# One of four weight sums per FFN block pair: made by adding transfers instead of by VectorE

## Chip, cores and metric

The kernel runs on one core of a Trainium2 chip. The metric is device time in microseconds (us) of one execution, as the median of several runs. VectorE is DVE in the profile, ScalarE is ACT, GpSimd is POOL, SyncE is SP, TensorE is PE (its weight loads PEld).

## The reference

One layer of a streaming encoder on x (512 tokens x 1024 features), all in float32. First a mixing sub-layer with three attention branches, which the change does not touch. Then the feed-forward network (FFN):

```
h = rmsnorm(x, g_ffn_pre)
gu = h @ w_ffn_in                                  # 1024 x (2 * 2816)
f = (silu(gu[:, :2816]) * gu[:, 2816:]) @ w_ffn_out
x = x + rmsnorm(f, g_ffn_post)
```

## The kernel before, in words

**Precision.** Each float32 operand is split into a high part (rounded to fp32r) and a low part (the rest). `split` (L73 to L75) makes them: ACT casts the high part (L74), DVE subtracts it from the source (L75). `passes` (L81 to L87) makes each product in three matmuls: high x high (L85), high x low (L86), low x high (L87).

**FFN, first matmul.** The 2816 columns of each half of w_ffn_in are cut into 22 blocks of 128. Block j of the gate half (g) and block j of the other half (u) make a pair; one pair is one row block of f. Pairs 0 to 2 are computed directly (`ffn`, L932). For pairs 3 to 21, 19 in all, `blocks` (L919) and `seven` (L886) use seven products instead of eight for the 2 x 2 block product of (g, u's two halves of the contraction) with the two halves of the tokens. Each product has four contraction chunks of three matmuls, so 84 matmuls per pair, each with 256 moving columns.

**The left sides** of the seven products come from `left_sides(j)` (L851). It loads g (512 KB, tag `wraw`, three buffers) and u (512 KB, tag `lraw`, two buffers), each 128 partitions x (8 contraction chunks x 128 columns), by SP's DMA queue. h[0] and h[1] are the first and last 512 columns, that is chunks 0 to 3 and 4 to 7. DVE makes four sums of 128 x 512 (L871): s12[h0] = u[h0] + u[h1]; s12[h1] = s12[h0] - g[h0]; s34[h0] = g[h0] - u[h0]; s34[h1] = g[h1] - s12[h1]. s12 and s34 are tiles of the tag `wl`, which has two buffers. Then g, s12 and s34 are split as a whole (128 x 1024) into tiles of 2048 columns (tag `w2`, four buffers, `wide` at L109), and u[h1] into a tile of tag `wh`. Split g gives products 1 and 2, split s12 gives 5 and 6, split s34 gives 7 and 3, split u[h1] gives 4.

**Order of the products.** `blocks` interleaves two pairs. In the steady stretch PE runs, per period: products 1 and 5 of pair j, 7 of pair j-1, 2 and 6 of pair j, 4 of pair j-1, 3 of pair j. Products 1, 2 and 3 read h2 itself (names bank<-h,w in the trace), 5, 6 and 7 read sums of h2 (bank<-act,w), 4 reads the `wh` tile (bank<-act,wh). Between them ACT copies banks out (L893, L895, L900) and DVE adds them (L898, L903, L907), and multiplies (L908, L911). Products 7 and 4 share a bank: product 4 may start when L907 has read it.

**What sets the order.** PE's order is the program's, written out by hand. For the FFN the order of the other engines' instructions and of the DMAs on each queue is set by the build's scheduler, from the dependencies and from when it expects a buffer to be free; each engine and each queue then runs in that order. A tile's buffer is free for its next use when every reader of the tile is done: s12's when ACT's cast and DVE's subtraction of it have ended.

**Before the stage.** `mix_out` (L785) ends the mixing sub-layer: post-norm, then the rows are transposed and split into h2 (L79 is DVE's part of that split, L359 the transpose on PE). The last of these transposes run inside `ffn`, beside the products of pair 0. POOL then adds the parts of h2 (L839) for the right sides of products 4 to 7. POOL has no work in the steady stretch of the stage.

Of the kernel before, what the change touches and what calls it, by code (L numbers as in the profile page):

```python
# [14 lines left out]
OP = mybir.AluOpType  # L15
AX = mybir.AxisListType

P = 128
# [4 lines left out]
DFF = 2816  # L23
# [24 lines left out]
class Layer:  # L48
# [802 lines left out]
    def left_sides(self, j):  # L851

        nc = self.nc
        g = self.load(self.a["w_ffn_in"][:, j * P:j * P + P], NK, P, "wraw")[0]
        u = self.load(self.a["w_ffn_in"][:, DFF + j * P:DFF + j * P + P], NK, P, "lraw")[0]
        x, h = {}, (slice(0, 512), slice(512, 1024))

        def cut(t, n, ps):
            for i, p in enumerate(ps):
                x[p] = tuple(t[:, c:c + 512] for c in (512 * i, n + 512 * i))  # L860

        def both(src, *ps):
            t = self.wide()
            self.split(t[:, 0:1024], t[:, 1024:2048], src)
            cut(t, 1024, ps)

        both(g, 1, 2)
        s12, s34 = self.big("wl", F32), self.big("wl", F32)
        for t, c, a, b, op in ((s12, 0, u[:, h[0]], u[:, h[1]], OP.add), (s12, 1, s12[:, h[0]], g[:, h[0]], OP.subtract),
                               (s34, 0, g[:, h[0]], u[:, h[0]], OP.subtract), (s34, 1, g[:, h[1]], s12[:, h[1]], OP.subtract)):  # L870
            nc.vector.tensor_tensor(t[:, h[c]], a, b, op=op)  # L871
        both(s12, 5, 6)
        both(s34, 7, 3)
        t = self.big("wh")
        self.split(t[:, h[0]], t[:, h[1]], u[:, h[1]])
        cut(t, 512, (4,))
        return x
# [123 lines left out]
```

## Time and profile before

| | us |
|---|---|
| median of 3 runs (912.41 to 913.62) | 912.44 |
| the profiled execution | 910.88 |
| its span, first to last instruction | 909.1 |
| seven-product stage in the trace, about | 592 to 781 |
| second matmul of the FFN (w_ffn_out), about | 781 to 897 |

All durations below come from the profiled execution. Its span is shorter than its time by what lies around the first and last instruction. Times in the trace count from the start of the span. "Idle before" in brackets names what the engine was waiting for. A DMA row of SPq shows the time in which SP issued the transfer, not the transfer.

### The profile page before, as it was taken

How to read it: one execution, taken by the hardware profiler on the slowest of the kernel's cores; microseconds unless marked ns; L12 is line 12 of the kernel's file. 1: busy time of each engine (PE TensorE's matmuls, PEld its weight loads, DVE VectorE, ACT ScalarE, POOL GpSimd, SP SyncE). 2: the span in 40 equal slices, each digit the busy share in tenths (PEclk: the TensorE clock that was granted, in tenths of full speed). 3: DMA queues.
4: the chain of work that ended last, by engine and by line, in shares of the span. 5: the costliest groups of instructions: out<-in, count | busy, mean ns of one | idle time of the engine just before them, and what ended most of it. 6: DMA issues, size and time to landing. Idle time of an engine off the chain costs nothing.

```text
span 909.1 us, 13518 instructions
## 1 busy us (share of the span) xinstructions
PE 888.3 (98%) x5146; PEld 780.1 (86%) x5146; DVE 641.5 (71%) x1120; ACT 458.6 (50%) x808; POOL 117.1 (13%) x153
## 2 busy tenths in 40 slices
PE   8999999999999999999999999899999999999997
PEld 7888888888888888888788888899999999888885
DVE  6589999953688976787563478788888887932215
ACT  6465674332666665666353355455555555811111
POOL 2000000020132304433212123400000000000000
PEclk9999999999999999999999999999999999999999
DMA  6523543454354433222483624213333334533002
GB/s 203 173 83 117 168 111 93 127 128 116 104 156 112 128 82 92 70 59 58 140 252 107 185 83 127 71 47 95 115 109 102 114 97 139 164 97 106 29 1 92
DMA packets 129541, 101.17 MB, mean 111 GB/s; under 512 B 4652, under 2 KB 115292, under 8 KB 129476
## 3 DMA queue, kind: packets, MB, share of 16 engines
q1 hardware_dynamic: 128884, 99.26, 37.9%
q10 hardware_dynamic: 592, 1.05, 0.3%
q8 instruction: 40, 0.66, 0.3%
q14 instruction: 25, 0.20, 0.1%
HBM read 93.73 MB, written 2.12 MB: 105 GB/s over the span
## 4 chain that ended last, share of the span: by engine, by line
PE 82%; DVE 10%; issue 3%; ACT 2%; POOL 2%; DMA 1%; POOLq 0%; DVEq 0%; ACTq 0%
PE bank L85 19%; PE bank L86 19%; PE bank L87 19%; PE bank L745 15%; DVE wl L75 3%; PE bank L545 2%; PE bank L560 1%; PE bank L179 1%; PE bank L178 1%; PE bank L209 1%; PE bank L211 1%; PE bank L210 1%; DMA lraw<-in_w_ffn_in_dram 1%; DVE e L632 1%; POOL rs L241 1%
## 5 line engine op out<-in xcount | busy, mean ns | idle before, releaser
L75 DVE TENSOR_TENSOR wl<-wraw,wh 128x1024 fp32r<-128x1024 f32 (+1 forms) x112 | 128.5, 1149 | 101.3 <-ACT wh L74 101.0
L74 ACT CAST wh<-wraw 128x1024 fp32r<-128x1024 f32 (+1 forms) x112 | 107.2, 959 | 139.3 <-PE bank L86 74.7
L85 PE MATMUL bank<-h,wh 128*128 128x512 f32 (+1 forms) x376 | 149.0, 396 | 0.0
L87 PE MATMUL bank<-h,wl 128*128 128x512 f32 (+1 forms) x376 | 145.4, 387 | 1.0 <-DVE wl L75 0.9
L86 PE MATMUL bank<-h,wh 128*128 128x512 f32 (+1 forms) x376 | 145.1, 386 | 0.0
L745 PE MATMUL bank<-w,act 128*128 128x512 f32 x360 | 89.0, 394 | 0.0
L87 PEld LDWEIGHTS bank<-h,wl 128*128 128x128 f32 x376 | 70.6, 188 | 15.8 <-DVE wl L75 1.7
L85 PEld LDWEIGHTS bank<-h,wh 128*128 128x128 f32 x376 | 71.0, 189 | 11.6 <-issue 0.2
L86 PEld LDWEIGHTS bank<-h,wh 128*128 128x128 f32 x376 | 70.9, 188 | 11.5
L745 PEld LDWEIGHTS bank<-w,act 128*128 128x128 f32 x360 | 67.4, 188 | 14.9
L745 PE MATMUL bank<-wh,act 128*128 128x512 f32 x240 | 72.5, 393 | 0.0
L85 PE MATMUL bank<-act,wh 128*128 128x256 f32 (+1 forms) x204 | 69.3, 340 | 0.7 <-DVE s L907 0.7
L86 PE MATMUL bank<-act,wh 128*128 128x256 f32 (+1 forms) x204 | 68.0, 334 | 0.0
L87 PE MATMUL bank<-act,w 128*128 128x256 f32 x228 | 64.2, 282 | 0.0
L86 PE MATMUL bank<-act,w 128*128 128x256 f32 x228 | 64.2, 281 | 0.0
L87 PE MATMUL bank<-h,w 128*128 128x256 f32 x228 | 64.2, 281 | 0.0
L86 PE MATMUL bank<-h,w 128*128 128x256 f32 x228 | 64.2, 281 | 0.0
L85 PE MATMUL bank<-act,w 128*128 128x256 f32 x228 | 64.2, 281 | 0.0
L85 PE MATMUL bank<-h,w 128*128 128x256 f32 x228 | 64.2, 281 | 0.0
L241 POOL TENSOR_TENSOR rs<-ms,mhalf 128x1 f32<-128x1 f32 x18 | 11.6, 646 | 387.4 <-DVE ms L240 383.7
L609 POOL TENSOR_TENSOR p<-toep,score 128x128 f32<-128x128 f32 (+3 forms) x32 | 30.4, 963 | 200.2 <-DVE score L518 102.9
L745 PEld LDWEIGHTS bank<-wh,act 128*128 128x128 f32 x240 | 45.0, 188 | 9.8
(190 smaller groups left out, 2109.5 us busy)
## 6 DMA issues: line engine op xcount, KB each, us to landing
wraw<-in_w_in_dram SPq DMA_DIRECT2D x64, 512.0 KB, 3.7
lraw<-in_w_ffn_in_dram SPq DMA_DIRECT2D x22, 512.0 KB, 4.0
wraw<-in_w_ffn_in_dram SPq DMA_DIRECT2D x22, 512.0 KB, 3.7
wraw<-in_w_ffn_out_dram SPq DMA_DIRECT2D x11, 512.0 KB, 3.5
lraw<-in_w_ffn_out_dram SPq DMA_DIRECT2D x11, 512.0 KB, 3.5
wraw<-in_w_mem_kv_dram SPq DMA_DIRECT2D x8, 512.0 KB, 3.7
lraw<-in_w_out_dram SPq DMA_DIRECT2D x6, 512.0 KB, 5.5
wraw<-in_w_out_dram SPq DMA_DIRECT2D x6, 512.0 KB, 3.9
```

Source lines behind the costliest of these rows:

```text
L74: self.nc.scalar.copy(hi, src)
L75: (eng or self.nc.vector).tensor_tensor(lo, src, hi.bitcast(F32), op=OP.subtract)
L85: self.nc.tensor.matmul(out, lhsT=sh, rhs=mh, start=first and i == 0, stop=False, **kw)
L86: self.nc.tensor.matmul(out, lhsT=sh, rhs=ml, start=False, stop=False, **kw)
L87: self.nc.tensor.matmul(out, lhsT=sl, rhs=mh, start=False, stop=last and i == n - 1, **kw)
L178: self.nc.tensor.matmul(out, lhsT=x, rhs=y[:, 0:n], start=True, stop=False)
L179: self.nc.tensor.matmul(out, lhsT=x, rhs=y[:, T:T + n], start=False, stop=True)
L209: self.nc.tensor.matmul(ps, lhsT=ah[:, s], rhs=wh[:, k2], start=st, stop=False)
L241: self.nc.gpsimd.tensor_tensor(r, ms, self.mhalf, op=OP.pow)
L545: self.nc.tensor.transpose(ps[:, c:c + P], p[i][:, j * P:(j + 1) * P], self.ident)
L609: nc.gpsimd.tensor_tensor(s, toep[0][:, 0:n][:, ::-1], self.mask[i], op=OP.add)
L745: self.nc.tensor.matmul(ps[c], lhsT=st_[:, s], rhs=mv_[:, 0, c * 512:(c + 1) * 512], start=f and k == order[0], stop=l and k == order[-1])
```

## The change

The first of the four sums, s12[h0] = u[h0] + u[h1], is no longer made by DVE. Chunks 0 to 3 of u are read a second time from w_ffn_in, on SP's queue, straight into s12[h0] (256 KB). Two transfers on POOL's queue then read chunks 4 and 5, and 6 and 7, of u from w_ffn_in (128 KB each), and add them into the two halves of s12[h0] in the on-chip buffer. u is still loaded whole as before, since s34[h0] and the split of u[h1] read it. The other three sums stay on DVE.

```diff
         s12, s34 = self.big("wl", F32), self.big("wl", F32)
-        for t, c, a, b, op in ((s12, 0, u[:, h[0]], u[:, h[1]], OP.add), (s12, 1, s12[:, h[0]], g[:, h[0]], OP.subtract),
+
+        for q, k, o, n, how in ((nc.sync, 0, 0, 4, {}), (nc.gpsimd, 4, 0, 2, {"accum_op": OP.add}),
+                                (nc.gpsimd, 6, 256, 2, {"accum_op": OP.add})):
+            q.dma_start(s12[:, o:o + n * P].rearrange("p (k c) -> p k c", c=P),
+                        self.a["w_ffn_in"][k * P:(k + n) * P, DFF + j * P:DFF + j * P + P]
+                        .rearrange("(k p) c -> p k c", p=P), **how)
+        for t, c, a, b, op in ((s12, 1, s12[:, h[0]], g[:, h[0]], OP.subtract),
                                (s34, 0, g[:, h[0]], u[:, h[0]], OP.subtract), (s34, 1, g[:, h[1]], s12[:, h[1]], OP.subtract)):
             nc.vector.tensor_tensor(t[:, h[c]], a, b, op=op)
```

## Rows read from the trace of the kernel before

**Rows 1.** The page, busy time of each engine.

```profile
PE 888.3 (98%) x5146; PEld 780.1 (86%) x5146; DVE 641.5 (71%) x1120; ACT 458.6 (50%) x808; POOL 117.1 (13%) x153
```

**Rows 2.** Windows: stretch; us, each engine's busy us (instructions), granted clock, DMA share, GB/s.

```profile
640.00:649.92 9.92, 9.92 (x86) 9.92 (x86) 8.44 (x14) 5.42 (x9) 0.00 (x0) 1.00 0.35 106
...
570.00:572.00 2.00, 0.00 (x0) 0.00 (x0) 2.00 (x4) 0.60 (x2) 0.00 (x0) 1.00 0.30 90
```

**Rows 3.** Waits of PE, 520 to 909 us: total us, times, longest.

```profile
PE bank L359 <- DVE h L79: 4.4, 2, 2.9
PE bank L85 <- DVE s L907: 0.7, 1, 0.7
```

**Rows 4.** Line 871, the removed sum, 540 to 600 us and 600 to 775 us.

```profile
L871 DVE TENSOR_TENSOR wl<-lraw x3: 689/692/694, 554.7 to 598.2; 128x512 f32<-128x512 f32 x3
...
L871 DVE TENSOR_TENSOR wl<-lraw x16: 691/693/695, 606.7 to 755.5; 128x512 f32<-128x512 f32 x16
```

**Rows 5.** Timeline of DVE, one period: start, duration, instruction, idle before.

```profile
645.16 1.22 DVE L75 TENSOR_TENSOR w<-wl,w 128x1024 fp32r<-128x1024 f32 x1
646.41 0.69 DVE L871 TENSOR_TENSOR wl<-lraw 128x512 f32<-128x512 f32 x1
...
649.42 0.69 DVE L871 TENSOR_TENSOR wl<-wl,wraw 128x512 f32<-128x512 f32 x1
...
652.52 0.43 DVE L907 TENSOR_TENSOR s<-bank,s 128x256 f32<-128x256 f32 x1 [1.21 <-PE bank L87]
...
654.88 0.42 DVE L898 TENSOR_TENSOR silu<-bank,s 128x256 f32<-128x256 f32 x1
655.21 1.22 DVE L75 TENSOR_TENSOR w<-wl,w 128x1024 fp32r<-128x1024 f32 x1
```

**Rows 6.** Timeline of ACT, the cast of the same s12.

```profile
644.06 1.05 ACT L74 CAST w<-wl 128x1024 fp32r<-128x1024 f32 x1 [0.41 <-PE bank L87]
```

**Rows 7.** Timeline of PE: first matmul of a product 5, and of a product 4.

```profile
649.49 0.28 PE L85 MATMUL bank<-act,w 128*128 128x256 f32 x1
...
655.15 0.28 PE L85 MATMUL bank<-act,wh 128*128 128x256 f32 x1
```

**Rows 8.** Timeline of SP's queue, the two issues of the same period.

```profile
644.93 0.37 SPq L95 DMA_DIRECT2D wraw<-in_w_ffn_in_dram  x1
649.53 0.37 SPq L95 DMA_DIRECT2D lraw<-in_w_ffn_in_dram  x1
```

**Rows 9.** DMA issues of the whole run: count, KB each, median us to landing.

```profile
wraw<-in_w_ffn_in_dram SPq DMA_DIRECT2D x22, 512.0 KB, 3.7
...
lraw<-in_w_out_dram SPq DMA_DIRECT2D x6, 512.0 KB, 5.5
...
wraw<-in_w_up_c_dram SPq DMA_DIRECT2D x8, 256.0 KB, 2.8
...
out_dram<-fin SPq DMA_DIRECT2D x4, 256.0 KB, 2.0
```

**Rows 10.** Timeline of POOL, 540 to 580 us: its longest and its shortest instruction there.

```profile
541.30 3.31 POOL L75 TENSOR_TENSOR act<-lraw,act 128x1024 fp32r<-128x1024 f32 x1 [2.48 <-ACT act L74]
...
551.76 0.55 POOL L241 TENSOR_TENSOR rs<-ms,mhalf 128x1 f32<-128x1 f32 x1
```

**Rows 11.** Timeline of DVE, subtractions of s12 of pair 4 and of pair 21.

```profile
596.93 1.23 DVE L75 TENSOR_TENSOR w<-wl,w 128x1024 fp32r<-128x1024 f32 x1 [0.58 <-ACT w L74]
...
764.20 1.22 DVE L75 TENSOR_TENSOR w<-wl,w 128x1024 fp32r<-128x1024 f32 x1
```

**Rows 12.** Timelines of DVE and of POOL where the FFN begins.

```profile
563.73 1.22 DVE L75 TENSOR_TENSOR w<-wl,w 128x1024 fp32r<-128x1024 f32 x1
...
569.25 0.69 DVE L871 TENSOR_TENSOR wl<-lraw 128x512 f32<-128x512 f32 x1
...
572.26 0.87 DVE L79 SCALAR_TENSOR_TENSOR h<-bank,cols,h 128x256 fp32r<-128x256 f32 x2
...
572.82 2.53 POOL L839 TENSOR_TENSOR act<-h 128x512 f32<-128x512 f32 x2 [6.21 <-DVE h L79]
```

## The prediction, made before the result was known

> **What bounds the kernel now.** I read the page's busy times first, then the waits of PE, then one block pair of the FFN stage engine by engine. On the page the reader is to see PE busy over 98% of the span [rows 1]; since the ends of matmuls are modelled, that alone says little, so the stage itself has to show whether PE ever waits. The window of one block pair in the steady stretch is 9.92 us long; PE is busy for all of it, DVE for 8.44, ACT for 5.42, POOL for nothing, the DMA engines for 0.35 [rows 2]. A block pair is 7 products of 4 x 3 matmuls, and 84 matmuls in 9.92 us are 0.118 us each, back to back. The list of PE's waits from the post-norm stage to the end confirms it: 0.7 us behind one VectorE addition (L907), and 4.4 us behind the splits of h (L79) where the FFN begins [rows 3]. So in the stage that the change edits, PE sets the time, and DVE work taken away there is worth nothing by itself. What can matter is whether the operands of the products still come in time.
>
> **What is removed.** The 128x512 addition u0+u1 (L871, output half 0 of s12) runs 3 times before 600 us and 16 times after, 19 in all [rows 4]. It costs 0.69 us each, 13 us of DVE. I cost this at nothing in the steady stretch: PE's 9.92 us per block pair hide it, and DVE had 1.48 us to spare per block pair already. If that cover went (if PE were faster), it would be worth at most 0.69 us per pair.
>
> **What is added, and where it queues.** Per block pair: a 256 KB read on SP's queue into half of the s12 buffer, then two accumulating transfers of 128 KB each on POOL's queue, which must wait for that read, and only then the second sum s12-g0, the cast and the subtraction that make the operands of product 5. The new thing is a loop through one buffer. The wl tag has two buffers, s12 and s34, so s12 of the next pair can be written only when the split of the present s12 has ended. Today that shows in the DVE timeline: the subtraction of s12 runs from 645.16 to 646.38, and the addition for the next pair starts at once, at 646.41 [rows 5]. Today the loop then has time: the second sum comes at 649.42, ACT's cast of an s12 at 644.06 [rows 6] and so of the next one 9.92 later, and the subtraction at 655.21 [rows 5]. PE first uses the result at 649.49 for the one that ended at 646.38 [rows 7]: 3.11 us of slack.
>
> How long may the loop be? The subtraction of s12 for the second seven-product pair starts at 596.93, that of the last at 764.20 [rows 11]; ends 598.16 and 765.42, 167.26 us for 17 loops. With the 3.11 us of slack, 170.4 us are free: 10.02 us per loop. Everything above it is paid 17 times.
>
> **The loop, term by term.** *Read.* A 256 KB weight load of just this form (four 512-byte rows per partition, w_up) lands 2.8 us after its issue, a 512 KB one 3.7 [rows 9], so 0.9 us belongs to 256 KB more. SP issues the load of a later g at 644.93 [rows 8], 1.45 us before the read can go; that load lands near 648.6, and the read's data comes behind it on the same queue: 648.6+0.9 = 649.5, which is 3.15 us after 646.38. Bounds 2.8 and 3.7; I take 3.15.
>
> *Accumulating transfers.* No transfer issued by POOL and none that adds is in this trace, so both parts are bounded. Issue: below, SP's 0.37 us [rows 8]; above, POOL's longest instruction, 3.31 us; I take its shortest, 0.55 us [rows 10], as an issue moves no data itself, and count it twice. Landing: below, 2.0 us as the shortest 256 KB row shows (a store); above, 5.5 us as the slowest weight load; I take 2.8 us, the 256 KB load, because an adding transfer of 128 KB reads 128 KB of weights and 128 KB of the buffer [rows 9]. SP issues a 512 KB load at 649.53 [rows 8], right beside them: I add 0.9 us, half of what such a load takes beyond the fixed part. Sum 2x0.55+2.8+0.9 = 4.8 us if the two overlap; bounds 2x0.37+2.0 = 2.7 and 2x3.31+5.5 = 12.1.
>
> The page "DMA: Bandwidth & Descriptors" of the Trainium skill (section "Anatomy of one DMA") fits a GpSimd-issued transfer as 2.0 us plus its bytes over 436 GB/s, so an estimate of 2.3 us for 128 KB; no run here shows it, and with it in place of 2.8+0.9 the loop would be 9.95 us and the sum of the change nothing.
>
> *Tail.* Second sum 0.69, then 1.10 from the start of the cast to the start of the subtraction (644.06 to 645.16), then 1.22: 3.0 us at least [rows 5, 6]. Above: if DVE keeps today's order, all that stands from the second sum at 649.42 to the end of the subtraction at 656.43, less the 1.21 us idle in it: 5.8 us [rows 5]. I take 3.4: the 0.42-us addition that stands right ahead of the subtraction today (654.88) stays there, the rest fits elsewhere.
>
> Loop: 3.15+4.8+3.4 = 11.35 us. 17 x 11.35 = 192.95, less 170.4: **22.6 us lost on PE**, as waits in front of product 5.
>
> **What waits behind the new waits.** On SP the read waits for DVE's subtraction; behind it stands the load issued now at 649.53, which comes later than the read anyway: nothing. On DVE the second sum waits for POOL's transfers; behind it stands L907 (652.52), whose end at 652.95 PE needs only at 655.15 [rows 5, 7]: 2.2 us of cover per pair, and once PE itself is late this cover grows: nothing more. On POOL nothing else runs in the stretch. The DMA engines' share of 0.35 for 1 MB per pair grows by at most 0.75 MB (with the buffer reads) to some 0.6: no bound. PE's clock: in a window where PE did nothing for 2 us the granted clock stays at 1.00, the 2.4 GHz level [rows 2]; I add nothing for stalls of 1 to 2 us.
>
> **Start of the stage.** The 4.4 us that PE waited for h L79 end behind five DVE instructions of the second pair (569.25 to 572.26), of which the removed addition is the first [rows 3, 12]: a gain of 0.6 us, and 1.8 if the two sums that need s12 fall behind L79 as well. Against this, s12's buffer there is free at 564.95 (563.73+1.22), the read lands at 568.1, the additions at 572.9; were the second sum still ordered ahead of L79, L79 would start 1.3 us later than now. POOL is idle for 6.21 us before its own additions at 572.82 [rows 12], so the two issues fit. I take zero, between -1.8 and +1.3.
>
> **The sum.** The profiled execution took 910.88 us (span 909.1 and 1.8 around it): 910.88+22.6 = 933.5. The median of the runs is 1.56 higher, 912.44, so 935.0 us.
>
> **Rivals.** (1) *No loss, the other side.* If the two transfers land within 3.45 us of the read (10.02-3.15-3.4), the loop hides under PE, and nothing moves but the start of the stage: 912.4, between 910.6 and 913.7. For it: 2.7 us is the lower bound, and stores land in 2.0. Against: the additions are two, behind a read, beside a 512 KB load. The point that decides is 3.45 us. The estimate from the Trainium skill's page above leads here, too. (2) *Faster.* The same, and in the start of the stage DVE reaches L79 1.8 us earlier and the 0.7 us at L907 goes as well: 909.9. For it: PE's idle time there is real and DVE-bound. Against: it needs the scheduler to put three instructions behind L79. (3) *A longer loop.* DVE keeps today's order around the second sum (5.8 for 3.4): loop 13.75, 17x13.75-170.4 = 63, so 976. Or the second transfer starts only when the first has landed, 2x(0.55+2.8)+0.9 = 7.6 for 4.8: loop 14.15, 70 us, so 983. For it: both go to one queue and one tile. Against: they write different columns, and the instruction order is set anew at build, with the transfers in it. With the upper bound of 12.1 us it would be 1059; I give that next to nothing, as no load here is near it but one group.
>
> **How the numbers follow.** Forecast (a loop of 10.2 to 12.8 us, 915 to 960) 0.49; rival 3, 0.21; rival 1, 0.22; rival 2, 0.08. A difference under 0.2% (1.8 us) cannot be told from none in this kernel. So faster 0.08, same 0.22, slower 0.70. The range goes from 910.5, which holds rival 1, to 972, which leaves out rival 2 and over half of rival 3: two in ten.
>
> **What would show it.** Right: the subtractions of s12 (DVE, w from wl) stand some 11.4 us apart instead of 9.92; PE's waits show 17 of over a microsecond behind L75; DVE idles before the second sum, released by a transfer into wl; the read lands about 3.1 us after its issue, the adding ones within 4.8 of it. Wrong: PE has no wait in the stage (rival 1), or loops of over 13 us (rival 3), where the two landings one after the other or the DVE order tell which. A clock below 1.00 in the stretch would be a cost that I left out.

## The result, and the profile after

The changed kernel takes 1019.36 us (1018.25 to 1021.01), against 912.42 us before on the same chip: a ratio of 1.118 (95% interval 1.115 to 1.120), 106.9 us more. The forecast was slower, 935 us, in a range of 910.5 to 972; the loss is nearly five times the 22.6 us forecast.

The page of the changed kernel: busy times, the queue of POOL's transfers, and the new issues (KB each, median us from issue to landing).

```profile
PE 926.6 (91%) x5146; PEld 814.4 (80%) x5146; DVE 627.6 (62%) x1101; ACT 453.8 (45%) x808; POOL 160.9 (16%) x191
...
q0 software_dynamic: 10336, 4.98, 4.0%
...
wl<-in_w_ffn_in_dram SPq DMA_DIRECT2D x19, 256.0 KB, 3.7
wl<-in_w_ffn_in_dram POOLq DMA_DIRECT2D x38, 128.0 KB, 3.5
```

Against [rows 1] DVE has lost 14 us of work, as the edit says, and PE is busy for 38 us longer with the same 5146 matmuls. POOL's transfers are no load worth the name: 4.0% of the DMA engines' time. So the loss is waiting, and a slower PE. The waits of PE from 540 to 890 us (total, times, longest):

```profile
PE bank L87 <- DVE w L75: 65.8, 18, 5.1
PE bank L359 <- DVE h L79: 5.5, 1, 5.5
PE bank L86 <- DVE h L79: 2.7, 1, 2.7
```

Where [rows 3] had one wait of 0.7 us behind L907 and nothing else in the steady stretch, there is now one wait per pair behind L75. One loop of the s12 buffer, from the end of one subtraction to the end of the next, in the timelines of SP, POOL, DVE and ACT (new line numbers: L872 the transfers, L877 the sums, L913 and L914 what were L907 and L908):

```profile
683.71 1.22 DVE L75 TENSOR_TENSOR w<-wl,w 128x1024 fp32r<-128x1024 f32 x1
...
683.88 0.37 SPq L95 DMA_DIRECT2D wraw<-in_w_ffn_in_dram  x1
684.96 0.37 SPq L872 DMA_DIRECT2D wl<-in_w_ffn_in_dram  x1
...
690.08 1.21 POOL L872 DMA_DIRECT2D wl<-in_w_ffn_in_dram  x1 [11.40 <-DVE act L914]
693.87 1.22 POOL L872 DMA_DIRECT2D wl<-in_w_ffn_in_dram  x1 [2.58 <-issue]
...
697.60 0.69 DVE L877 TENSOR_TENSOR wl<-wl,wraw 128x512 f32<-128x512 f32 x1 [8.04 <-DMA wl<-in_w_ffn_in_dram]
698.21 1.22 DVE L75 TENSOR_TENSOR w<-wraw,w 128x1024 fp32r<-128x1024 f32 x1
...
698.45 1.04 ACT L74 CAST w<-wl 128x1024 fp32r<-128x1024 f32 x1 [8.80 <-DVE wl L877]
...
700.28 1.22 DVE L75 TENSOR_TENSOR w<-wl,w 128x1024 fp32r<-128x1024 f32 x1
```

The reader is to follow the links, each of which starts when the one before ends. The subtraction of s12 ends at 684.93, SP issues the read at 684.96; POOL issues the first adding transfer at 690.08, the second at 693.87; the second sum runs at 697.60; the next subtraction ends at 701.50. That is 16.57 us where [rows 5] has 10.05 us (646.38 to 656.43), and it is in three parts: 5.1 us until POOL's first issue, 7.5 us for the two additions, 3.9 us for the tail. On DVE the subtraction of g (698.21) stands behind the waiting second sum, and product 1 of the next pair waits for that: PE's wait names L75.

Two things in these rows mislead. POOL's first issue is put down to L914, since several semaphores are waited for and that one came last. In the loops where the trace gives the read's landing, 10 of 17, POOL starts 0.63 to 0.72 us after it (here landing 4.4 us after the issue, 689.36, and 0.72 us more), while L914 ends 0.4 us ahead of POOL's start in one loop, 15 us ahead in another, and in a third is still running: it is the read. And the 2.58 us ahead of the second issue end by nothing that the profile shows ("issue"); in the program that instruction has no wait at all, and DVE is idle from 689.55 to 697.60. The first transfer lands 3.5 us after its issue at 690.08, so at 693.6, and the second issue follows 0.3 us later; it does so in all 17 loops.

The second sums of the steady stretch, with the time of the first and the last of 17, give the mean period: (871.3-617.4)/16 = 15.87 us.

```profile
L877 DVE TENSOR_TENSOR wl<-wl,wraw x17: 691/693/693, 617.4 to 871.3; 128x512 f32<-128x512 f32 x17
```

By the prediction's own account 17 loops of 15.87 us less the 170.4 us that are free are 99.4 us. The rest, some 7 us, has to come from before the first loop. The two traces show both parts in one line each: PE's matmuls of L85 in products 1, 2 and 3, with the start of the first and of the last, before and after the change.

```profile
L85 PE MATMUL bank<-h,w x228: 280/281/282, 591.4 to 776.7; 128*128 128x256 f32 x114
...
L85 PE MATMUL bank<-h,w x228: 275/282/421, 599.7 to 884.1; 128*128 128x256 f32 x114
```

The stage starts 8.3 us late, and from there takes 284.4 us in place of 185.3: 99.1 us more.

### The profile page after: what moved, and what is told of

Its sections match the earlier page's. It is cut to its first block, busy times and chain, and to the rows that moved or that the text cites. A ratio compares the mean times of both kernels' runs of the same rounds, so it can differ in the third digit from the quotient of the medians.

```text
span 1016.7 us, 13672 instructions
## 1 busy us (share of the span) xinstructions
PE 926.6 (91%) x5146; PEld 814.4 (80%) x5146; DVE 627.6 (62%) x1101; ACT 453.8 (45%) x808; POOL 160.9 (16%) x191
## 3 DMA queue, kind: packets, MB, share of 16 engines
q0 software_dynamic: 10336, 4.98, 4.0%
## 4 chain that ended last, share of the span: by engine, by line
PE 61%; DVE 14%; DMA 11%; issue 8%; POOL 4%; ACT 2%; DVEq 0%; POOLq 0%; ACTq 0%
PE bank L745 14%; PE bank L87 13%; PE bank L85 13%; PE bank L86 12%; DMA wl<-in_w_ffn_in_dram 9%; DVE w L75 3%; DVE wl L75 3%; POOL wl L872 2%; DVE wl L877 2%; PE bank L545 2%; PE bank L560 1%; PE bank L179 1%; PE bank L178 1%; PE bank L209 1%; PE bank L211 1%
## 5 line engine op out<-in xcount | busy, mean ns | idle before, releaser
L75 DVE TENSOR_TENSOR wl<-wraw,wh 128x1024 fp32r<-128x1024 f32 (+1 forms) x112 | 128.6, 1149 | 101.5 <-ACT wh L74 101.1
L85 PE MATMUL bank<-h,wh 128*128 128x512 f32 (+1 forms) x376 | 149.0, 396 | 0.0
L87 PE MATMUL bank<-h,w 128*128 128x256 f32 x228 | 74.4, 326 | 65.4 <-DVE w L75 65.4
L87 PEld LDWEIGHTS bank<-h,w 128*128 128x128 f32 x228 | 50.6, 222 | 68.9 <-DVE w L75 68.9
L74 ACT CAST w<-wl 128x1024 fp32r<-128x1024 f32 x38 | 39.6, 1046 | 140.4 <-DVE wl L877 139.4
L877 DVE TENSOR_TENSOR wl<-wl,wraw 128x512 f32<-128x512 f32 x19 | 13.1, 692 | 120.1 <-DMA wl<-in_w_ffn_in_dram 115.8
L872 POOL DMA_DIRECT2D wl<-in_w_ffn_in_dram x38 | 46.4, 1222 | 252.2 <-DMA wl<-in_w_ffn_in_dram 108.6
L85 PEld LDWEIGHTS bank<-h,wh 128*128 128x128 f32 x376 | 71.0, 189 | 11.7 <-issue 0.2
L85 PE MATMUL bank<-act,w 128*128 128x256 f32 x228 | 71.6, 314 | 0.0
L86 PE MATMUL bank<-act,w 128*128 128x256 f32 x228 | 70.7, 310 | 0.0
L87 PE MATMUL bank<-act,w 128*128 128x256 f32 x228 | 70.0, 307 | 0.4 <-DVE w L75 0.4
L85 PE MATMUL bank<-act,wh 128*128 128x256 f32 (+1 forms) x204 | 69.2, 339 | 1.1 <-DVE s L913 1.1
L86 PE MATMUL bank<-h,w 128*128 128x256 f32 x228 | 70.1, 307 | 0.0
L85 PE MATMUL bank<-h,w 128*128 128x256 f32 x228 | 69.9, 306 | 0.0
```

The lines of the kernel that those rows point to most:

```text
L74: self.nc.scalar.copy(hi, src)
L75: (eng or self.nc.vector).tensor_tensor(lo, src, hi.bitcast(F32), op=OP.subtract)
L85: self.nc.tensor.matmul(out, lhsT=sh, rhs=mh, start=first and i == 0, stop=False, **kw)
L86: self.nc.tensor.matmul(out, lhsT=sh, rhs=ml, start=False, stop=False, **kw)
L87: self.nc.tensor.matmul(out, lhsT=sl, rhs=mh, start=False, stop=last and i == n - 1, **kw)
L872: q.dma_start(s12[:, o:o + n * P].rearrange("p (k c) -> p k c", c=P), self.a["w_ffn_in"][k * P:(k + n) * P, DFF + j * P:DFF + j * P + P] . ...
```

## The experiments

The theory after the result (A in the expectations): a loop through the s12 buffer, in which the second adding transfer is held back until the first has landed, plus some 8 us at the start of the stage. The rivals are given with each run. Runs that needed room on the chip moved four tiles of the attention stage (`score0` to `score3`, `diag`) to a pool that is closed before the FFN; the last experiment is the control for that.

**More room for the descriptors of POOL's transfers.**

```diff
-    nc = bacc.Bacc("TRN2", target_bir_lowering=False, num_devices=1, dynamic_dma_scratch_size=1024)
+    nc = bacc.Bacc("TRN2", target_bir_lowering=False, num_devices=1, dynamic_dma_scratch_size=4096)
```

> The changed kernel with four times the on-chip memory for the descriptors of POOL's transfers (4096 bytes per partition for 1024); the score and diag tiles move to the pool that is closed before the FFN, to make room. Theory A (the second adding transfer is held until the first has landed, for want of room for its descriptors): the 2.6 us between the end of the first issue and the start of the second fall to under 0.3 us, the loop of 16.6 us shortens to 14.0, and the time falls by 17 x 2.6 = 44 us to about 975 us. Rival B (POOL's transfers go one after the other whatever the room): the gap stays at 2.6 us and the time at 1019 us.

Measured: 970.44 us, ratio 1.065 (1.063 to 1.066). The timeline of POOL shows both issues as one piece of 2.44 us, without a gap; below it are the second sums of the stretch and the matmuls of L85.

```profile
699.06 2.44 POOL L872 DMA_DIRECT2D wl<-in_w_ffn_in_dram  x2 [11.40 <-DVE s L913]
...
L877 DVE TENSOR_TENSOR wl<-wl,wraw x17: 691/693/694, 609.4 to 825.0; 128x512 f32<-128x512 f32 x17
...
L85 PE MATMUL bank<-h,w x228: 276/281/420, 594.6 to 836.7; 128*128 128x256 f32 x114
```

The period is (825.0-609.4)/16 = 13.48 us, 2.4 us shorter, and the time is 48.9 us shorter. The gap was the room for descriptors. Of what is left, 58.3 us, the account puts 17 x 13.48 - 170.4 = 58.8 us into the loops. The trace has 56.8 us there (242.1 for 185.3) and 3.2 us ahead of the stage, together the 60.2 us between the two profiled executions (971.03 and 910.88). So 5.1 us of the gain come from the start of the stage.

**Plain transfers in place of adding ones.**

```diff
-        for q, k, o, n, how in ((nc.sync, 0, 0, 4, {}), (nc.gpsimd, 4, 0, 2, {"accum_op": OP.add}),
-                                (nc.gpsimd, 6, 256, 2, {"accum_op": OP.add})):
+        for q, k, o, n, how in ((nc.sync, 0, 0, 4, {}), (nc.gpsimd, 4, 0, 2, {}),
+                                (nc.gpsimd, 6, 256, 2, {})):
```

> The two transfers on POOL's queue overwrite instead of adding, so s12[h0] holds chunks 4 to 7 of u and not the sum. Theory A (room for descriptors: an adding transfer needs two reads for each write, a plain one one): the second issue follows the first within 0.3 us, the loop is 16.6 - 2.6 = 14.0 us or, if a plain transfer also lands sooner (2.8 for 3.6), 13.2, and the time 960 to 978 us. Rival B (any two transfers of POOL follow one another): gap 2.6 us, 1005 to 1020 us.

Measured: 945.75 us, ratio 1.038 (1.035 to 1.041), better than either theory said. Timeline of POOL, the sums, the issues with their landing, and the queue of POOL's transfers:

```profile
699.75 1.44 POOL L872 DMA_DIRECT2D wl<-in_w_ffn_in_dram  x2 [11.09 <-DMA wl<-in_w_ffn_in_dram]
...
L877 DVE TENSOR_TENSOR wl<-wl,wraw x17: 691/693/694, 606.6 to 796.8; 128x512 f32<-128x512 f32 x17
...
wl<-in_w_ffn_in_dram POOLq DMA_DIRECT2D x38, 128.0 KB, 2.7
...
q0 software_dynamic: 1824, 4.98, 1.8%
```

With the small room of the changed kernel there is no gap, as theory A has it, so it is the adding form that fills the room. The last line shows how the forms differ: the same bytes go in 1824 packets, 48 for each of the 38 transfers, where the adding ones took 10336, 272 each. Two costs of adding that I had not priced come on top: the issue takes 1.22 us for an adding transfer and 0.72 for a plain one, and the landing 4.0 us (overlapped, in the run before) for 2.7. The period is 11.89 us: 17 x 11.89 - 170.4 = 31.7 us, measured 33.6. In the trace the matmuls of L85 run from 592.8 to 808.8 us, so 30.7 us are lost in the stage and 1.4 ahead of it.

**A third buffer for s12 and s34.**

```diff
-    BUFS = dict(h=8, act=22, wraw=3, wh=2, wl=2, lraw=2, pt=3, fin=4)
+    BUFS = dict(h=8, act=22, wraw=3, wh=2, wl=3, lraw=2, pt=3, fin=4)
```

> The changed kernel with three wl buffers for two (the same tiles moved to make room, descriptor memory as in the changed kernel). Theory A (the loss is the loop through the one s12 buffer): a read can go some 7.7 us earlier, when the buffer of the s34 before is free, so 17.7 us are free for a loop of 16.6: no wait of PE behind L75 in the steady stretch, granted clock 1.00, and 912 to 922 us, the remainder being the start of the stage. Rival B (the transfers themselves, their load on the DMA engines or POOL's issue cost the time): PE goes on waiting, over 960 us.

Measured: 1000.26 us, ratio 1.097 (1.095 to 1.099): theory A's bounds missed by 78 us, and rival B's met. The chain of waits of this kernel, one loop in order of time (start, us, what; some short links are left out):

```profile
697.30 1.13 DVE w L75
...
698.46 2.93 DMA wl<-in_w_ffn_in_dram
...
702.07 5.16 DMA wl<-in_w_ffn_in_dram
707.23 3.83 issue
711.06 0.20 DVE wl L877
...
711.67 0.41 DVE act L917
712.09 1.14 DVE w L75
...
713.25 3.03 DMA wl<-in_w_ffn_in_dram
```

and the second adding transfer of that loop in the timeline of POOL, which the chain has inside the 3.83 us of "issue":

```profile
707.55 1.22 POOL L872 DMA_DIRECT2D wl<-in_w_ffn_in_dram  x1 [4.27 <-issue]
```

The chain has no PE in it: it is still a loop of buffer, read, additions and DVE, of 14.8 us. The read now goes into the buffer of the s34 before; but that s34's subtraction (712.09 in the next round) stands on DVE behind the second sum that waits for the transfers (711.06). The order of DVE's instructions closed the loop again, one tile further on. So a spare buffer is not yet a decoupling, and the run could not tell A from B. It does show two things by itself. The gap follows the landing: the first adding transfer takes 5.2 us to land here, at 707.23, and the second is issued 0.3 us after that, with a gap of 4.27 us for 2.58. And the read, here no longer right behind a load of 512 KB on SP's queue, lands after 2.9 us; in the changed kernel, 1.1 us behind such a load, its median is 3.7.

**A tile of its own for the transfers.** Three buffers of 128x512, filled by the read and the additions; s12 keeps its second half alone.

```diff
+        wa = self.late.tile([P, 512], F32, name="wa", tag="wa", bufs=3)
...
-            q.dma_start(s12[:, o:o + n * P].rearrange("p (k c) -> p k c", c=P),
+            q.dma_start(wa[:, o:o + n * P].rearrange("p (k c) -> p k c", c=P),
...
-        for t, c, a, b, op in ((s12, 1, s12[:, h[0]], g[:, h[0]], OP.subtract),
+        for t, c, a, b, op in ((s12, 1, wa, g[:, h[0]], OP.subtract),
...
-        both(s12, 5, 6)
+        t = self.wide()
+        self.split(t[:, 0:512], t[:, 1024:1536], wa)
+        self.split(t[:, 512:1024], t[:, 1536:2048], s12[:, h[1]])
+        cut(t, 1024, (5, 6))
```

> The changed kernel, but the read and the two adding transfers fill a tile of their own (128x512, three buffers) in place of the half of s12; s12 keeps only its second half, and its split is made in two halves. Same transfers, same room for descriptors. Theory A (the loss is a loop in which a buffer has to be given back before its next transfers start, and three buffers of their own put the transfers two pairs ahead): 29.8 us are free for read and additions of about 12 us, no wait of PE behind L75 in the steady stretch, sums 9.92 us apart, 908 to 925 us, where all above 912 comes from POOL's queue at the start of the stage. Rival B (two adding transfers per 9.92 us load POOL or the DMA engines too much): periods of over 11 us, over 930 us.

Measured: 939.28 us, ratio 1.030 (1.029 to 1.032). The number is rival B's, the trace is not. The waits of PE from 300 us on, the timeline of POOL around 490 us, far ahead of the FFN, and the matmuls of L85:

```profile
PE bank L85 <- ACT wh L74: 18.0, 1, 18.0
PE bank L359 <- DVE act L251: 6.9, 1, 6.9
...
486.42 1.21 POOL L873 DMA_DIRECT2D wa<-in_w_ffn_in_dram  x1 [2.69 <-issue]
490.23 1.22 POOL L873 DMA_DIRECT2D wa<-in_w_ffn_in_dram  x1 [2.60 <-issue]
490.98 1.76 POOL L721 TENSOR_TENSOR act<-act,gate 128x512 f32<-128x512 f32 x1
...
L85 PE MATMUL bank<-h,w x228: 281/281/281, 619.6 to 804.9; 128*128 128x256 f32 x114
```

No wait in the steady stretch is over a microsecond any more, with the small room and its gaps. Instead, the three free buffers let the scheduler put six adding transfers on POOL's queue in the middle of the merge of the attention branches, and the merge's addition (L721) stood behind them: 18.0 us of PE in one wait, and 6.9 in another. The last line settles where the whole loss lies: the stage starts 28.2 us late and takes the 185.3 us of the kernel before, so nothing is lost in it.

**The same, with the transfers kept out of the earlier stages.** Pairs 5 to 21 as above; on POOL their transfers are queued behind L839; pairs 3 and 4 get the read with DVE's addition.

```diff
+        own = j >= 5
...
+        if own:
+            with self.tc.issue_after(self.last_add.ins):
+                for k, o in ((4, 0), (6, 256)):
+                    nc.gpsimd.dma_start(dst(o, 2), src(k, 2), accum_op=OP.add)
```

> As the run with a tile of its own, but the adding transfers serve pairs 5 to 21 only and are queued on POOL behind its additions for the right sides (L839); pairs 3 and 4 get the read with DVE's addition. 17 first sums are made by 34 adding transfers. Theory A (the transfers cost nothing once their buffer is free two pairs ahead and nothing of the earlier stages stands behind them on POOL): no wait of PE in the steady stretch, sums 9.92 us apart, 908 to 911 us, as with the read alone, although DVE has 17 x 0.69 us less to add: that work is worth nothing there. Rival B (the 27 us of the run before come from the transfers themselves, somewhere else): 925 us or more.

Measured: 909.11 us, ratio 0.996 (0.995 to 0.997). The waits of PE from 520 us on, one period's window, and two issues of POOL in it:

```profile
PE bank L359 <- DVE h L79: 3.0, 2, 1.5
PE bank L85 <- DVE s L923: 0.7, 1, 0.7
...
640.00:649.92 9.92, 9.92 (x86) 9.92 (x85) 7.91 (x13) 5.52 (x9) 1.97 (x3) 1.00 0.71 160
...
639.50 1.21 POOL L878 DMA_DIRECT2D wa<-in_w_ffn_in_dram  x1 [5.05 <-DVE wl L881]
643.28 1.22 POOL L878 DMA_DIRECT2D wa<-in_w_ffn_in_dram  x1 [2.57 <-issue]
```

All 34 adding transfers are still there, with the gap of 2.57 us between two, and cost nothing: PE is busy for all of the 9.92 us. They bring nothing either: pairs 3 and 4 get the read here, and the run with that read alone, further down, takes 908.99 us. DVE's work in the window has fallen from 8.44 us [rows 2] to 7.91, and nothing came of it. The DMA engines' share has doubled to 0.71, over the 0.6 that the prediction had as its most, without harm.

**The start of the stage alone.** Pairs 3 and 4 as in the changed kernel, the others as before.

```diff
+        for q, k, o, n, how in () if not (j < 5) else ((nc.sync, 0, 0, 4, {}), (nc.gpsimd, 4, 0, 2, {"accum_op": OP.add}),
+                                (nc.gpsimd, 6, 256, 2, {"accum_op": OP.add})):
...
```

> Pairs 3 and 4 as in the changed kernel, pairs 5 to 21 as before. Theory A (of the loss, about 8 us arise before the first loop, because the adding transfers stand on POOL's queue ahead of its splits and of the rs of the post-norm): 918 to 922 us. Rival B (the 17 loops hold all the loss): 911 to 914 us.

Measured: 919.39 us, ratio 1.008 (1.007 to 1.010), 7.1 us lost. The waits of PE, and the timeline of POOL:

```profile
PE bank L359 <- DVE h L79: 5.6, 1, 5.6
PE bank L86 <- DVE h L79: 2.6, 1, 2.6
...
543.63 1.37 POOL L872 DMA_DIRECT2D wl<-in_w_ffn_in_dram  x1 [4.98 <-PE bank L359]
544.62 2.81 POOL L75 TENSOR_TENSOR act<-lraw,act 128x1024 fp32r<-128x1024 f32 x1
550.27 1.24 POOL L872 DMA_DIRECT2D wl<-in_w_ffn_in_dram  x1 [2.83 <-issue]
```

POOL's split of a u block (L75), which started at 541.30 before [rows 10], stands behind the first adding transfer, which waits for its read, and starts at 544.62. What follows on POOL, the rs of the post-norm among it, is late with it. These 7.1 us and the 99.4 of the loops make 106.5 of the 106.9 us. (In this trace the stage starts 8.2 us late and then takes the time that it took before.)

**The read alone,** with DVE adding u[h1] into it: for all pairs, for pairs 3 and 4, and for pairs 5 to 21.

```diff
-        for t, c, a, b, op in ((s12, 0, u[:, h[0]], u[:, h[1]], OP.add), (s12, 1, s12[:, h[0]], g[:, h[0]], OP.subtract),
+        for q, k, o, n, how in ((nc.sync, 0, 0, 4, {}),):
...
+        for t, c, a, b, op in ((s12, 0, s12[:, h[0]], u[:, h[1]], OP.add), (s12, 1, s12[:, h[0]], g[:, h[0]], OP.subtract),
```

> Only the read on SP's queue is kept; DVE adds u[h1] into it, so DVE has as many sums as before. Theory A (a loop under 10.0 us is hidden): read 4.4 to 5.1 us, addition 0.6, then 3.9 as in the changed kernel, so 8.9 to 9.6 us, and 911 to 916 us. Rival B (a second read of the same weights, or the order on SP's queue, costs by itself): over 925 us.

> The read with DVE's addition for pairs 3 and 4 only, the rest as before. Theory A (the 3.2 us that the kernel with the read alone gains come from another order of DVE's instructions at the start of the stage, where PE waits for L79): 908 to 910 us. Rival B (they come from the steady stretch or its end): 911.5 to 913 us.

> The counterpart: the read with DVE's addition for pairs 5 to 21, pairs 3 and 4 as before. Theory A: 911.5 to 913 us, as PE has no wait there to lose. Rival B: 908 to 910 us.

Measured: 908.94 us for all pairs, ratio 0.997 (0.996 to 0.998), a little below theory A's bounds; 908.99 for pairs 3 and 4, ratio 0.997 (0.996 to 0.998); 912.46 for the rest, ratio 1.001 (1.000 to 1.002). In the steady stretch the read is hidden, though DVE now idles for it (the kernel with all pairs, timeline of DVE). The gain is at the start: below it are PE's wait and DVE's first split of h for the run with pairs 3 and 4.

```profile
648.47 0.69 DVE L876 TENSOR_TENSOR wl<-wl,lraw 128x512 f32<-128x512 f32 x1 [0.65 <-DMA wl<-in_w_ffn_in_dram]
```

```profile
PE bank L359 <- DVE h L79: 2.9, 2, 1.5
...
570.38 0.87 DVE L79 SCALAR_TENSOR_TENSOR h<-bank,cols,h 128x256 fp32r<-128x256 f32 x2
```

L79 starts at 570.38 in place of 572.26 [rows 12], although DVE has the same number of sums: the scheduler has ordered them otherwise. PE waits 1.5 us less for it than in [rows 3]. Between the profiled executions (908.90 and 910.88) the gain is 2.0 us; the medians are 3.3 us apart, as the kernel before spreads over 910.5 to 913.5 us. That spread goes with PE's granted clock: of the 16 runs of the kernel before that stand beside these, those of 910.5 to 910.7 us show a mean of 0.998, those of 911.7 to 912.5 us 0.996 or 0.997, and the two of 913.5 us 0.995. The trace of the control below, a run of 912.16 us, shows one place where it falls: PE's wait for L79 is 2.9 us long in it as before, and these are the 4 us after that wait, first in the kernel before and then in the control.

```profile
572.00:576.00 4.00, 3.20 (x27) 3.20 (x28) 2.46 (x6) 1.43 (x3) 2.53 (x2) 1.00 0.73 217
...
572.00:576.00 4.00, 3.19 (x16) 3.19 (x17) 1.88 (x5) 0.95 (x2) 2.50 (x2) 0.57 0.73 212
```

At a granted clock of 0.57 PE gets through 16 matmuls where it had 27. With the read at pairs 3 and 4 the wait is 1.5 us, and every run of that kernel is at 0.998 or 0.999. So the median gains more than the shorter wait.

**The control for the moved tiles.**

```diff
-        self.diag = self.const.tile([P, 512], F32, name="diag")
+        self.diag = self.att.tile([P, 512], F32, name="diag")
```

> The kernel before with only the score and diag tiles moved to the pool that is closed before the FFN: the control for the runs that needed the room. Both theories: 911.5 to 913 us.

Measured: 912.29 us, ratio 1.000 (0.999 to 1.001). The move plays no part in the times.

## Why the prediction was wrong, point by point

**What bounds the kernel: right.** DVE's work in the stage is worth nothing. The run with the decoupled transfers has 17 of the 19 additions taken from DVE, and equals the run that took none.

**The loop, and the time that is free: right.** The direction, the loop through the one s12 buffer and the 10.02 us hold. The account, 17 times the period less 170.4 us, gives what the stage loses in three kernels with periods from 11.89 to 15.87 us to within 2 us (99.4 for 99.1, 58.8 for 56.8, 31.7 for 30.7), and where the period is 9.92 nothing is lost. (The limit of rival 1, 10.02-3.15-3.4, is 3.47 and not 3.45; nothing hangs on it.)

**The adding transfers, 4.8 us: the step that failed.** They take 7.5 us. I let the two overlap, and put "one starts when the other has landed" among the rivals, at 7.6 us, with the argument that they write different columns. No dependency holds the second; room for descriptors does, and with four times the room the gap is gone. Of the 4.5 us by which the loop of 15.87 exceeds 11.35, this is 2.7, and over 17 loops 46 of the 84 us by which the forecast fell short. The price of one landing, 2.8 us, was the plain one's (2.7 measured); an adding one takes 3.5, and its issue 1.22 for my 0.55. The estimate of 2.3 us from the fit on the page "DMA: Bandwidth & Descriptors" of the Trainium skill (section "Anatomy of one DMA") is too short here even for the plain transfer, at 2.7; the measured 2.7 and 3.5 decide.

**The read, 3.15 us: too small.** Its landing is 3.7 us, behind a 512 KB load as argued, but issued only 1.1 us after it and not 1.45. And a link was missing: from the landing to POOL's issue another 0.65 us pass. Together some 1.2 us per loop.

**The tail, 3.4 us: 3.9 measured** in every one of the 17 loops, as the last of the four sums (s34) and L904 get in front of the subtraction. These shortfalls, 2.7, 1.2 and 0.5 us, make 4.4 of the 4.5 us.

**Behind the wait on DVE: wrong in place.** I looked at L907 alone. The scheduler moved that ahead of the waiting sum and left the subtraction of g behind it, so PE's wait is in product 1 and not in product 5. The time does not hang on it, as the loop sets it.

**The start of the stage, zero: 7.1 us lost.** I placed the transfers of pair 4 on an idle POOL, and gave those of pair 3 no thought. It is these that were queued ahead of POOL's two splits. The first transfer of pair 4 did not find POOL idle either: in the run of the start alone it is issued at 568.84, ahead of the last rs of the post-norm, which starts at 569.64 for 565.15 before.

**PE's clock: wrong, and hidden.** I read from a window with one stall of 2 us [rows 2] that the clock stays at 1.00, the 2.4 GHz level. That was the luck of that trace: after the same stall the granted clock of the control fell to 0.57. With a stall in every period it falls again and again. Windows of the changed kernel:

```profile
600.00:610.00 10.00, 10.00 (x88) 10.00 (x87) 7.03 (x9) 5.19 (x9) 0.02 (x1) 1.00 0.09 27
...
710.00:720.00 10.00, 5.26 (x30) 5.06 (x29) 5.96 (x9) 3.11 (x5) 1.22 (x1) 0.67 0.29 66
720.00:730.00 10.00, 8.06 (x67) 7.86 (x66) 2.20 (x5) 2.08 (x4) 2.44 (x2) 0.98 0.49 104
```

Just before the loops begin the granted clock is 1.00; from 630 to 880 us it is between 0.66 and 0.99 in every such window, so part of PE's work runs at the 1.2 GHz level. That is why PE's waits (66 us) are less than the loss: the same matmuls take longer and fill some of the wait. Every link of the loop is on SP, POOL, the DMA engines, ACT or DVE; none waits for PE in the trace, and the account without the clock (99.4 us) leaves nothing of the stage's 99.1 us to it. So the slower clock costs nothing here, as far as the trace tells; no run held the clock.

## What to carry to other kernels

When work moves from an engine to transfers that fill a reused buffer, add up the whole loop from the buffer's release to its next release, every landing, wait and issue in it, and compare it with the period: an engine's spare time does not enter. A further buffer helps only if no queue in order closes the loop again, so look at which instruction stands in front of the one that gives the buffer back, and at what a queue that now waits had been doing before. And where an instruction starts late with no wait in the program, as POOL's second transfer did, look for a resource that can be made larger; here it was the room for descriptors.

## What the runs showed of the hardware

- Two adding transfers of 128 KB in a row, each of 256 rows of 512 bytes, do not fit at once in 1024 bytes per partition of descriptor memory: POOL starts the second 2.6 us after the end of the first's issue, 0.3 us after the first has landed; where that landing took 5.2 us (three buffers), the gap was 4.3. With 4096 bytes, or with plain transfers in 1024, there is no gap.
- An adding transfer of this form goes in 272 packets, a plain one in 48 (10336 and 1824 for 38).
- POOL spends 1.22 us on issuing an adding transfer and 0.72 us on a plain one of the same size; by the medians they land after 3.5 us (adding, one after the other), 4.0 us (adding, two at once) and 2.7 us (plain, two at once).
- From the landing of a transfer to the issue on POOL that waits for it, 0.6 to 0.7 us pass (10 loops of the changed kernel).
- After one and the same wait of PE, 2.9 us long, the granted clock stayed at 1.00 in one run and fell to 0.57 over the next 4 us in another.
